# Two-layer hybrid decoder trunk on one core: the next layer's opening placed in the hand-made PE order of the last rows, the first stage reordered, the last products shared by ScalarE

## The chip, the cores and the metric

One core of one Trainium2 chip runs the whole program. The metric is the device time of the program in microseconds (us), lower is better. Engines: PE is TensorE, DVE is VectorE, ACT is ScalarE, POOL is GpSimd, SP is SyncE, which here only starts transfers.

## The reference

The trunk has DEPTH = 2 layers over a sequence of 512 tokens of 1024 float32 values (four tiles of 128 tokens). Each layer is, cut to its frame:

```
h = rms_norm(x, norm_g[l])
proj = h @ w_in[l]                      # 1024 -> 4376
q, k_c, v_c, k_s, v_s, k_w, v_w, g_lin, z_nsa, u_lru, z_lru, glu_a, glu_b, z_conv = split(proj)
gates = sigmoid(g_lin + b_gate[l])
y_nsa  = nsa_attention(...)             # compressed, selected and window branch, gated
y_lru  = rg_lru(...)
y_conv = conformer_conv(...)
mixed  = concat([y_nsa * silu(z_nsa), y_lru * silu(z_lru), y_conv * silu(z_conv)])
x = x + mixed @ w_out[l]                # 1536 -> 1024
```

and behind the second layer `rms_norm(x, final_g)` is the output. rms_norm is x / sqrt(mean(x*x) + 1e-6) * g over the 1024 values of a token.

## The kernel before

Matrices are multiplied in three products each: both operands are split in a high half (a cast by ACT, `cast` L149) and a low half (a subtraction by DVE, `lower` L152), and hi·hi, lo·hi and hi·lo are summed in one accumulator. So each weight tile takes a load (SP), a cast (ACT, tiles `whi`, `ow` or `wv`) and a subtraction (DVE, `wlo`, `ow` or `wv`) before all its products can run. All weights go through one pair of load buffers: `raw_tile` (L155) has two buffers of 1 MB, so a load waits until the casts and subtractions of the tile two places before it are done. SP starts its transfers in order.

**Opening of a layer** (L240 to L338): the weights of the values v_s, v_w and the gates are loaded (`wv`, 1024 rows in two pieces of 768 and 256 rows), split by `value_weights(j)` in parts j = 0, 1 (128x840) and 2 (128x560). Part 2 is kept in buffers that the queries (`QS`, tags qs0 and qs1) of the layer before used. Each token tile is normalised (`rms_norm` L220: squares on ACT with row sums, small sums on DVE, a power on POOL, a step of Newton's method on DVE, and the product with g), turned by eight PE transposes (`turned` L268, `hnat` to `H`, copied high by ACT and low by DVE), and multiplied by wv in 24 products (L321 to L338). In layer 0 the order of ACT and DVE in this stage is written out by hand in START (L44). In layer 1 the order is a scheduler's.

**End of a layer** (`last_rows`, L853): the attention of token tile 0 and the output products of the attention part for all tiles. The order of PE there is written out by hand in LAST_ROWS (L41): `s g b` are scores, `t g b` transposes of the weights P, `v g b` their products with the values, `o g` opens an output accumulator, and `r t n` are the 12 products of token tile t with half n of w_out (`out_rows` L417), added to x by DVE. The weights of half n are loaded and split where the first `r t n` of that half is met (`rows` L879, `out_weights` L406), so r30 stands for the load of half 0, r21 for that of half 1. The instructions of the other engines, and the places of loads in SP's queue, follow from the order in which the steps are written and from a scheduler. The opening of layer 1 was written behind all that, so its transposes and values came behind r00 on PE, but for what the scheduler moved.

**End of the program** (L922): each tile is normalised with final_g and stored; tile 0 is last, in two halves.

Of the kernel before, what the change touches and what calls it, by code (L numbers as in the profile page):

```python
# [1 line left out]

# [13 lines left out]
T = 512  # L16
# [21 lines left out]

LAST_ROWS = "s10 c s00 r30 s01 r20 d r10 t00 o0 t01 s11 v00 v01 r21 t10 t11 r31 o1 v10 v11 r11 r01 r00"  # L41


START = "q3 c3 p30 p31 q2 t30 c2 t31 p20 w0 p21 q1 t20 c1 w1 t21 p10 q0 p11 w2 t10 c0 t11 p00 p01 t00 t01"  # L44


@with_exitstack
def tile_hybrid_trunk(ctx, tc, x_in, positions, norm_g, w_in, b_gate, cmp_pos, cmp_w1, cmp_w2, lru_conv_w,
# [100 lines left out]
    def cast(out, in_):  # L149
        S.copy(out, in_)  # L150
# [58 lines left out]
                n += 1  # L209
        return p  # L210

    def rsqrt(y, v4):

        s = work.tile([128, 2], F32, name="nw", tag="nw", bufs=4)
        G.tensor_tensor(y, v4, power, op=OP.pow)  # L215
        V.tensor_scalar(s[:, 0:1], v4, -1.0, None, op0=OP.mult)
        V.scalar_tensor_tensor(s[:, 1:2], y, s[:, 0:1], y, op0=OP.mult, op1=OP.mult)
        V.scalar_tensor_tensor(y, s[:, 1:2], 3.0, y, op0=OP.add, op1=OP.mult)

    def rms_norm(x, gb, name, halves=False):  # L220

        y = pair(name)
        ss = work.tile([128, 4], F32, name="ss", tag="ss", bufs=4)
        for n in range(2):
            S.activation(y[:, n], x[:, n], AF.Square, accum_out=ss[:, n:n + 1])
            if n == 0:
                V.tensor_scalar(ss[:, 2:3], ss[:, 0:1], 4.0 / DM, 4.0 * EPS, op0=OP.mult, op1=OP.add)
        V.scalar_tensor_tensor(ss[:, 3:4], ss[:, 1:2], 4.0 / DM, ss[:, 2:3], op0=OP.mult, op1=OP.add)
        rsqrt(ss[:, 2:3], ss[:, 3:4])
        for n in (slice(0, 1), slice(1, 2)) if halves else (slice(0, 2),):  # L230
            V.scalar_tensor_tensor(y[:, n], x[:, n], ss[:, 2:3], gb[:, n], op0=OP.mult, op1=OP.mult)
        return y

    def load_g(ap):
# [2 lines left out]
        return g  # L237


    def layer(l, X):  # L240
        if l == 0:
            grow = pair("grow")[0:1].rearrange("p a c -> p (a c)")
            SP.dma_start(out=grow, in_=norm_g[0:1, :])
            load_x(0, X, (3, 2))
        else:
            gb = load_g(norm_g[l])
        wv = [w_cols(l, (COL["v_s"], 128), (COL["v_w"], 152), rows=rows) for rows in ((0, 6), (6, 2))]
        if l == 0:
            load_x(0, X, (1, 0))
        bg = work.tile([128, 24], F32, name="bg", tag="bg", bufs=1)  # L250
        SP.dma_start(out=bg, in_=bass.AP(tensor=b_gate.tensor, offset=b_gate[l].offset, ap=[[0, 128], [1, 24]]))

        def chan(name, src2d, n):
            t = main.tile([128, 4, n], F32, name=name, tag=name, bufs=1)
# [4 lines left out]
                PE.transpose(p[:, ct, :n], nat[:n, ct * 128:(ct + 1) * 128], ident[:n, :n])  # L259
            V.tensor_copy(t, p[:, :, :n])  # L260
            return t


        H2 = [[quad(f"H{w}{a}") for a in range(2)] for w in range(2)]
        Hh, Hl = [[H2[w][k // 4][:, k % 4, :] for k in range(8)] for w in range(2)]
        WV = [None] * 8

        def turned(t, h, n):  # L268
            p = psum.tile([128, 4, 128], F32, name="pt", tag="tr", bufs=2)
            for k in range(4):  # L270
                PE.transpose(p[:, k, :], h[:, n, k * 128:(k + 1) * 128], ident)
            sl = slice(t * 128, (t + 1) * 128)
            S.copy(H2[0][n][:, :, sl], p)
            V.tensor_tensor(H2[1][n][:, :, sl], p, H2[0][n][:, :, sl].bitcast(F32), op=OP.subtract)

        def value_weights(j):

            n = 3 if j < 2 else 2
            src = wv[j // 2][:, 3 * j % 6:3 * j % 6 + n, :]
            hi, lo = (main.tile([128, 4 if j == 2 else 2, 512], F32R, name="wv",  # L280
                                tag=(f"kh{j}", f"kl{j}")[w] if j < 2 else f"qs{w}", bufs=1) for w in range(2))
            hi, lo = (w.rearrange("p a b -> p (a b)")[:, :n * 280].rearrange("p (k c) -> p k c", k=n) for w in (hi, lo))
            cast(hi, src)
            lower(lo, src, hi)
            WV[3 * j:3 * j + n] = [(hi[:, k], lo[:, k]) for k in range(n)]

        if l == 0:

            hs, ss = {}, {}
            gp = [psum.tile([128, 512], F32, name="acc", tag="ps", bufs=3) for n in range(2)]  # L290
            for n in range(2):
                PE.matmul(gp[n], one, grow[:, n * 512:(n + 1) * 512], start=True, stop=True)

            def squares(t):
                hs[t] = pair("hnat")
                ss[t] = work.tile([128, 4], F32, name="ss", tag="ss", bufs=4)
                S.activation(hs[t], X[t], AF.Square, accum_out=ss[t][:, 0:1])

            def chain(t):
                V.tensor_scalar(ss[t][:, 3:4], ss[t][:, 0:1], 4.0 / DM, 4.0 * EPS, op0=OP.mult, op1=OP.add)  # L300
                rsqrt(ss[t][:, 2:3], ss[t][:, 3:4])

            def product(t, n):
                V.scalar_tensor_tensor(hs[t][:, n], X[t][:, n], ss[t][:, 2:3], gp[n], op0=OP.mult, op1=OP.mult)

            steps = dict(q=squares, c=chain, p=product, t=lambda t, n: turned(t, hs[t], n), w=value_weights)
            with tc.manual_schedule(engines={mybir.EngineType.Activation, mybir.EngineType.DVE}):
                for step in START.split():
                    steps[step[0]](*map(int, step[1:]))
        else:  # L310
            for j in range(3):
                value_weights(j)
            for t in (2, 3, 1, 0):
                SP.dma_start(out=saved[t], in_=X[t])
                h = rms_norm(X[t], gb, "hnat", t == 0)
                for n in range(2):
                    turned(t, h, n)


        VV, GT = [None] * 4, [None] * 4  # L320
        for t in (2, 3, 1, 0) if l else (3, 2, 1, 0):  # L321
            p = acc()
            sl = slice(t * 128, (t + 1) * 128)
            m = 0
            for k in range(8):
                for w, h in ((WV[k][0], Hh), (WV[k][0], Hl), (WV[k][1], Hh)):
                    PE.matmul(p[:, 0:280], h[k][:, sl], w, start=m == 0, stop=m == 23)  # L327
                    m += 1
            v = main.tile([128, 4, 2, 64], F32R, name="vv", tag="vv", bufs=4)
            pv = p[:, 0:256].rearrange("p (b d) -> p b d", b=4)  # L330
            S.copy(v[:, :, 0, :], pv)
            V.tensor_tensor(v[:, :, 1, :], pv, v[:, :, 0, :].bitcast(F32), op=OP.subtract)
            VV[t] = v
            gt = main.tile([128, 24], F32, name="gt", tag="gt", bufs=4)
            V.tensor_tensor(gt, p[:, 256:280], bg, op=OP.add)
            S.activation(gt, gt, AF.Tanh, scale=0.5)
            V.tensor_scalar(gt, gt, 0.5, 0.5, op0=OP.mult, op1=OP.add)
            GT[t] = gt  # L338


        dww = chan("dww", conv_dw_w[l], 31)
# [382 lines left out]
        def do_attn():  # L724
# [127 lines left out]

            def last_rows(X):  # L853
                new_mn(0)
                with tc.manual_schedule(engines={mybir.EngineType.PE}):
                    W, PTS, Ps, PO = {}, {}, {}, {}

                    def soft(g, b):
                        Ps[g, b] = weights_of(0, 4 * g, 4, b)

                    def turn(g, b):
                        PTS[g, b] = [big("pt", F32R).rearrange("p (k r q) -> p k r q", k=1, r=4) for _ in range(2)]
                        turned_weights(0, Ps[g, b], 4, PTS[g, b])

                    def comp():
                        PO["c"] = compressed_weights(0)

                    def turn_comp():
                        PO["c"] = turned_compressed(PO["c"])

                    def open_po(g):
                        PO[g] = new_po(g, PO["c"])

                    def vals(g, b):
                        values(PO[g], 0, g, b, PTS[g, b], b == 1)
                        if b == 1:
                            merged(PO[g], 0, g)

                    def rows(t, n):  # L879
                        if n not in W:  # L880
                            W[n] = out_weights(0, n, n == 1)
                        out_rows(X, t, n, W[n], MN[t])

                    steps = dict(s=soft, t=turn, c=comp, d=turn_comp, o=open_po, v=vals, r=rows)
                    for step in LAST_ROWS.split():
                        steps[step[0]](*map(int, step[1:]))

            return last_rows

# [22 lines left out]
        do_pw2()  # L912
        last_rows = do_attn()
        out_proj(X, 8, MC)
        last_rows(X)
        return X

    X = [None] * 4
    for l in range(DEPTH):
        X = layer(l, X)  # L920

    gb = load_g(final_g)  # L922
    for t in (2, 3, 1, 0):
# [31 lines left out]
```

## Time and profile before

| | us |
|---|---|
| median of 3 runs | 787.17 |
| lowest, highest | 785.59, 787.50 |
| the profiled execution, its own time | 786.09 |
| its span, first to last instruction | 784.3 |
| mean granted TensorE clock | 0.997 |

How to read it: the profile is one execution. A timeline row gives start, busy time, engine, line of the kernel, the operation, out<-in tiles (buffer numbers left out), the count of instructions that follow each other, and in brackets the idle time of the engine before the row with what ended it. Rows of PE overlap, since products are pipelined; from start to start is the measure of what they cost. A clock of 1.00 is 2.4 GHz, 0.50 is 1.2 GHz.

### The profile page before, as it was taken

Reading aid. Unit: us, or ns where it says so; the run is one execution under the profiler, and the core shown is the slowest. Engines: PE = TensorE matmul, PEld = TensorE weight load, DVE = VectorE, ACT = ScalarE, POOL = GpSimd, SP = SyncE. Lnnn points to the kernel's source line nnn. Section 1 sums busy time; section 2 is a strip of 40 time slices with the busy share of each in tenths; the row PEclk is TensorE's granted clock in tenths of the full one; section 3 lists DMA queues with packets and bytes.
Section 4 is the critical chain, followed back from the end, with each engine's and each line's share of the span. In section 5 each row is a group of like instructions: output and inputs, shape, how many; then the busy total and the mean of one; then the engine's idle time right before and its main releaser. Section 6 shows DMA issues by size and latency. Waiting matters only on the chain.

```text
span 784.3 us, 10943 instructions
## 1 busy us (share of the span) xinstructions
PE 755.0 (96%) x3816; PEld 604.8 (77%) x3816; DVE 676.4 (86%) x1243; ACT 452.1 (58%) x889; POOL 101.7 (13%) x179
## 2 busy tenths in 40 slices
PE   6999999999999999999989999999999999999995
PEld 4988887677887777888788888776788787778874
DVE  5889999999997788978873999999999778888766
ACT  5443666784336466667642348669534466676663
POOL 2000000000001132433210000000000103434240
PEclk9999999999999999999999999999999999999998
DMA  6433285656432200103531334771854140010002
GB/s 192 155 108 107 57 223 133 167 164 222 142 128 81 81 2 1 54 1 86 169 105 54 107 89 126 188 199 32 275 165 160 53 145 17 1 55 2 1 28 107
DMA packets 68245, 82.01 MB, mean 105 GB/s; under 512 B 6601, under 2 KB 56841, under 8 KB 68190
## 3 DMA queue, kind: packets, MB, share of 16 engines
q1 hardware_dynamic: 68190, 81.31, 33.9%
q8 instruction: 30, 0.49, 0.3%
q14 instruction: 25, 0.20, 0.1%
HBM read 67.67 MB, written 4.19 MB: 92 GB/s over the span
## 4 chain that ended last, share of the span: by engine, by line
PE 78%; DVE 9%; ACT 6%; issue 4%; POOL 2%; DMA 0%; POOLq 0%; DVEq 0%; SPq 0%; ACTq 0%
PE acc L208 43%; PE acc L423 10%; PE po L813 5%; PE pt L798 3%; PE acc L718 3%; PE acc L327 3%; PE ps L779 2%; ACT P L787 2%; PE ps L780 2%; DVE wlo L153 1%; DVE cv L381 1%; PE pt L630 1%; POOL P L791 1%; ACT pt L800 1%; PE pt L735 1%
## 5 line engine op out<-in xcount | busy, mean ns | idle before, releaser
L208 PE MATMUL acc<-H,whi 128*128 128x512 f32 x1024 | 325.5, 398 | 0.0
L208 PEld LDWEIGHTS acc<-H,whi 128*128 128x128 f32 x1024 | 191.1, 188 | 47.5 <-issue 1.9
L208 PE MATMUL acc<-H,wlo 128*128 128x512 f32 x512 | 203.7, 399 | 2.1 <-DVE wlo L153 2.1
L150 ACT CAST whi<-raw 128x1024 fp32r<-128x1024 f32 x102 | 106.5, 1050 | 159.4 <-PE acc L208 130.1
L381 DVE SCALAR_TENSOR_TENSOR cv<-sg,dww,cv 128x493 f32<-128x493 f32 (+18 forms) x240 | 165.9, 737 | 0.9
L153 DVE TENSOR_TENSOR wlo<-raw,whi 128x1024 fp32r<-128x1024 f32 x102 | 124.8, 1225 | 22.1 <-ACT whi L150 21.2
L208 PEld LDWEIGHTS acc<-H,wlo 128*128 128x128 f32 x512 | 96.2, 188 | 27.3 <-DVE wlo L153 3.4
L791 POOL TENSOR_SCALAR P<-P,hm,gt 128x384 f32<-128x384 f32 (+3 forms) x128 | 81.1, 643 | 135.7 <-DVE hm L789 127.1
L787 ACT ACTIVATE P<-ps,hm 128x384 f32<-128x384 f32 (+3 forms) x128 | 67.0, 532 | 15.7 <-DVE hm L784 15.1
L801 DVE TENSOR_TENSOR pt<-pt 128x512 fp32r<-128x512 f32 (+1 forms) x88 | 54.2, 638 | 12.9 <-ACT pt L800 11.8
L784 DVE TENSOR_REDUCE hm<-ps 128x1 f32<-128x384 f32 (+3 forms) x88 | 54.8, 634 | 8.2 <-PE ps L781 4.4
L813 PE MATMUL po<-pt,vv 128*128 128x256 f32 (+1 forms) x304 | 58.0, 304 | 1.1 <-DVE pt L801 0.7
L215 POOL TENSOR_TENSOR mv<-mv,power 128x1 f32<-128x1 f32 x8 | 4.2, 544 | 418.1 <-DVE mv L680 418.1
L800 ACT CAST pt<-pt 128x512 fp32r<-128x512 f32 (+1 forms) x88 | 46.0, 548 | 21.4 <-PE pt L798 18.8
L813 PEld LDWEIGHTS po<-pt,vv 128*128 128x128 f32 x304 | 44.7, 189 | 9.8 <-ACT pt L800 4.6
L798 PE MATMUL pt<-ident,P 128*128 128x128 f32 x320 | 47.6, 275 | 1.6 <-POOL P L791 1.3
L779 PE MATMUL ps<-KH,QS 128*128 128x384 f32 (+3 forms) x128 | 45.5, 367 | 0.8 <-ACT P L787 0.6
L798 PEld LDWEIGHTS pt<-ident,P 128*128 128x128 f32 x320 | 36.9, 140 | 6.0 <-POOL P L791 4.1
L780 PE MATMUL ps<-KL,QS 128*128 128x384 f32 (+3 forms) x128 | 40.5, 328 | 0.0
L327 PE MATMUL acc<-wv,H 128*128 128x280 f32 x192 | 30.6, 313 | 2.5 <-ACT wv L150 1.5
L425 DVE TENSOR_TENSOR x<-x,acc 128x512 f32<-128x512 f32 x48 | 32.4, 677 | 0.8 <-PE acc L423 0.4
L423 PE MATMUL acc<-whi,mn 128*128 128x512 f32 x96 | 31.1, 406 | 0.0
(233 smaller groups left out, 1213.3 us busy)
## 6 DMA issues: line engine op xcount, KB each, us to landing
raw<-in_w_in_dram SPq DMA_DIRECT2D x30, 1024.0 KB
raw<-in_w_out_dram SPq DMA_DIRECT2D x12, 1024.0 KB
raw<-in_cmp_w_dram SPq DMA_DIRECT2D x8, 1024.0 KB
x<-in_x_dram SPq DMA_DIRECT2D x8, 512.0 KB
raw<-in_w_in_dram SPq DMA_DIRECT2D x4, 512.0 KB
QS<-rs SPq DMA_DIRECT2D x8, 256.0 KB
QS<-ru SPq DMA_DIRECT2D x8, 256.0 KB
KH<-rs SPq DMA_DIRECT2D x8, 256.0 KB
```

The lines of the kernel that those rows point to most:

```text
L150: S.copy(out, in_)
L153: (eng or V).tensor_tensor(out, in_, hi.bitcast(F32), op=OP.subtract)
L208: PE.matmul(p, w[k], h[k], start=n == 0, stop=n == 23)
L381: V.scalar_tensor_tensor(a[:, s:], u[:, :T - s], dww[:, ct, j:j + 1], a[:, s:], op0=OP.mult, op1=OP.add)
L423: PE.matmul(p, h[:, k], w, start=m == 0, stop=m == 11)
L779: PE.matmul(sc[:, r, :], q, KH[g][:, b, :L], start=r == 0, stop=False)
L780: PE.matmul(sc[:, r, :], q, KL[g][:, b, :L], start=False, stop=False)
L784: V.tensor_reduce(hm[:, 0, :nh], sc, axis=AX.X, op=OP.min)
L787: S.activation(P[:, r * L:(r + 1) * L], sc[:, r, :], AF.Exp, scale=-1.0, bias=hm[:, 0, r:r + 1], accum_out=hm[:, 1, r:r + 1])
L791: G.tensor_scalar(P[:, r * L:(r + 1) * L], P[:, r * L:(r + 1) * L], hm[:, 2, r:r + 1], GA[i][:, h0 + r, 1 + b:2 + b], op0=OP.mult, op1=OP. ...
L798: PE.transpose(pt[:, kb, :], P[:, kb * 128:(kb + 1) * 128], ident)
L813: PE.matmul(po, v, PT[w][:, kb].rearrange("p r q -> p (r q)"), start=False, stop=last and kb == i and w == 1)
```

## The change

- LAST_ROWS has the opening of the next layer in it: `L` are its loads, `W` the splits of wv, `N t` the norm of tile t, `T t` its eight transposes, `V t` its 24 products. The functions of the opening move into `opening`, which hands these steps to `last_rows` of layer 0. In layer 1 there is no next layer, and the new steps are skipped.
- START is reordered and its step c (row sums and root) is split in c and e; in layer 0, x of tile 3 is loaded first, g by ACT's queue, and wv in three pieces, of 384, 384 and 256 rows.
- rms_norm of the last tile of a norm: squares of half 1 first; x·g of half 1 is made before the root is known, and ACT multiplies it by the root while DVE makes half 0.

```diff
-LAST_ROWS = "s10 c s00 r30 s01 r20 d r10 t00 o0 t01 s11 v00 v01 r21 t10 t11 r31 o1 v10 v11 r11 r01 r00"
-START = "q3 c3 p30 p31 q2 t30 c2 t31 p20 w0 p21 q1 t20 c1 w1 t21 p10 q0 p11 w2 t10 c0 t11 p00 p01 t00 t01"
+LAST_ROWS = "s10 c s00 r30 s01 r20 d r10 t00 o0 t01 s11 L v00 v01 r21 N2 t10 W t11 r31 N3 o1 v10 v11 T2 r11 N1 r01 " \
+            "T3 r00 N0 V2 T1 V3 T0 V1 V0"
+START = "q3 c3 e3 p30 p31 q2 c2 w0 e2 t30 p20 t31 q1 p21 c1 w1 e1 t20 p10 t21 q0 p11 c0 w2 e0 t10 p00 t11 p01 t00 t01"
...
-    def rms_norm(x, gb, name, halves=False):
+    def rms_norm(x, gb, name, last=False):
...
-        for n in range(2):
+        for n in ((1, 0) if last else (0, 1)):
             S.activation(y[:, n], x[:, n], AF.Square, accum_out=ss[:, n:n + 1])
-            if n == 0:
-                V.tensor_scalar(ss[:, 2:3], ss[:, 0:1], 4.0 / DM, 4.0 * EPS, op0=OP.mult, op1=OP.add)
+            if n == last:
+                V.tensor_scalar(ss[:, 2:3], ss[:, n:n + 1], 4.0 / DM, 4.0 * EPS, op0=OP.mult, op1=OP.add)
+                if last:
+                    V.tensor_tensor(y[:, 1], x[:, 1], gb[:, 1], op=OP.mult)
...
-        for n in (slice(0, 1), slice(1, 2)) if halves else (slice(0, 2),):
-            V.scalar_tensor_tensor(y[:, n], x[:, n], ss[:, 2:3], gb[:, n], op0=OP.mult, op1=OP.mult)
+        n = slice(0, 1 if last else 2)
+        V.scalar_tensor_tensor(y[:, n], x[:, n], ss[:, 2:3], gb[:, n], op0=OP.mult, op1=OP.mult)
+        if last:
+            S.activation(y[:, 1], y[:, 1], AF.Copy, scale=ss[:, 2:3])
...
+    def opening(l, X):
...
+        def loads():
+            load_wv(0, 6)
+            load_wv(6, 2)
+            o.gb = load_g(norm_g[l])
+            load_bg()
...
+        if l:
+            o.steps = dict(L=loads, W=weights, N=norm, T=turned_tile, V=values)
+            return o
...
+        load_x(0, X, (3,))
+        grow = pair("grow")[0:1].rearrange("p a c -> p (a c)")
+        S.dma_start(out=grow, in_=norm_g[0:1, :])
+        load_x(0, X, (2,))
+        load_wv(0, 3)
+        load_wv(3, 3)
+        load_x(0, X, (1, 0))
+        load_wv(6, 2)
+        load_bg()
...
             def last_rows(X):
                 new_mn(0)
+                nxt = opening(l + 1, X) if l + 1 < DEPTH else None
...
                     steps = dict(s=soft, t=turn, c=comp, d=turn_comp, o=open_po, v=vals, r=rows)
+                    if nxt:
+                        steps |= nxt.steps
                     for step in LAST_ROWS.split():
-                        steps[step[0]](*map(int, step[1:]))
+                        if step[0] in steps:
+                            steps[step[0]](*map(int, step[1:]))
+                return nxt
```

SP's queue at the end of layer 0. Before (lines of the kernel before); 128x4x512 is a half of w_out, 6x128 and 6x152 are the first piece of wv, 2x128 and 2x152 the second, 8x256 the first weights of layer 1's projection:

```order
L409 DMA raw<-in_w_out_dram 128x4x512 x4
L708 DMA pwr<-in_conv_w_pw_dram 128x2x256 x2
L409 DMA raw<-in_w_out_dram 128x4x512
L708 DMA pwr<-in_conv_w_pw_dram 128x2x256 x2
L409 DMA raw<-in_w_out_dram 128x4x512
L165 DMA raw<-in_w_in_dram 128x6x128
L165 DMA raw<-in_w_in_dram 128x6x152
L236 DMA g<-in_norm_g_dram 128x1024
L165 DMA raw<-in_w_in_dram 128x2x128
L165 DMA raw<-in_w_in_dram 128x2x152
L165 DMA raw<-in_w_in_dram 128x8x256 x2
```

The same place with the change:

```order
L447 DMA raw<-in_w_out_dram 128x4x512 x4
L746 DMA pwr<-in_conv_w_pw_dram 128x2x256 x2
L447 DMA raw<-in_w_out_dram 128x4x512
L746 DMA pwr<-in_conv_w_pw_dram 128x2x256 x2
L168 DMA raw<-in_w_in_dram 128x6x128
L168 DMA raw<-in_w_in_dram 128x6x152
L168 DMA raw<-in_w_in_dram 128x2x128
L168 DMA raw<-in_w_in_dram 128x2x152
L251 DMA g<-in_norm_g_dram 128x1024
L447 DMA raw<-in_w_out_dram 128x4x512
L168 DMA raw<-in_w_in_dram 128x8x256 x2
```

The load of the second half of w_out, which r21 to r01 read, stood ahead of both pieces of wv and now stands behind them.

ACT in the same place, before; `whi` and `ow` here are the two casts of that second half:

```order
L150 CAST whi<-raw 128x1024
L800 CAST pt<-pt 128x512
L828 CAST mn_3162<-m 128x256
L800 CAST pt<-pt 128x512
L150 CAST ow<-raw 128x1024
L824 COPY oe<-po 64x256
```

and with the change, where the casts of that half stand behind those of wv and ahead of the squares of the next norm:

```order
L153 CAST wv<-raw 128x560
L153 CAST wv<-raw 128x840
L862 COPY oe<-po 64x256
L825 ACTIVATE P,hm<-ps,hm 128x128 x4
L862 COPY oe<-po 64x256
L866 CAST mn_3537<-m 128x256
L153 CAST whi<-raw 128x1024
L153 CAST ow<-raw 128x1024
L236 ACTIVATE hnat,ss<-x_1867 128x512
```

The two casts (and DVE's two subtractions with them) were done in the middle of the attention of tile 1; now they stand at the place of r21.

PE behind the last product of r00, before:

```order
L271 MATMUL pt<-ident,hnat 128x128 x6
L327 MATMUL acc<-wv,H_3868 128x280
L271 MATMUL pt<-ident,hnat 128x128 x4
L327 MATMUL acc<-wv,H_3870 128x280
L327 MATMUL acc<-wv,H_3868 128x280
L271 MATMUL pt<-ident,hnat 128x128 x4
```

and with the change, from the output products of tile 1 on, at the step T3:

```order
L461 MATMUL acc<-ow,mn_3537 128x512
L278 MATMUL pt<-ident,hnat 128x128 x8
L461 MATMUL acc<-whi,mn_3537 128x512
L461 MATMUL acc<-whi,mn_3538 128x512
L461 MATMUL acc<-wlo,mn_3537 128x512
```

Transposes of tiles 2 and 3 now stand among output products, and each tile's values run as one group of 24.

## Rows read from the trace of the kernel before

**Rows 1.** The page: busy time of each engine, share, instructions

```profile
PE 755.0 (96%) x3816; PEld 604.8 (77%) x3816; DVE 676.4 (86%) x1243; ACT 452.1 (58%) x889; POOL 101.7 (13%) x179
```

**Rows 2.** Timeline of PE at the layer boundary (columns as told above)

```profile
375.80 1.28 PE L813 MATMUL po<-pt,vv 128*128 128x512 f32 x4
376.91 0.62 PE L423 MATMUL acc<-whi,mn 128*128 128x512 f32 x2
...
379.69 1.72 PE L798 MATMUL pt<-ident,P 128*128 128x128 f32 x7
381.67 0.33 PE L798 MATMUL pt<-ident,P 128*128 128x128 f32 x1 [0.26 <-POOL P L791]
...
394.52 0.82 PE L271 MATMUL pt<-ident,hnat 128*128 128x128 f32 x6
396.23 0.40 PE L327 MATMUL acc<-wv,H 128*128 128x280 f32 x1 [0.89 <-ACT H L273]
397.88 0.66 PE L271 MATMUL pt<-ident,hnat 128*128 128x128 f32 x4 [1.25 <-DVE H L274]
...
401.07 0.60 PE L271 MATMUL pt<-ident,hnat 128*128 128x128 f32 x4
401.43 1.78 PE L327 MATMUL acc<-wv,H 128*128 128x280 f32 x12
403.40 0.66 PE L271 MATMUL pt<-ident,hnat 128*128 128x128 f32 x4 [0.18 <-DVE H L274]
...
405.13 8.41 PE L327 MATMUL acc<-wv,H 128*128 128x280 f32 x63
```

**Rows 3.** Timeline of SP's queue: the load of w_out's second half

```profile
315.13 0.37 SPq L409 DMA_DIRECT2D raw<-in_w_out_dram  x1
```

**Rows 4.** Timeline of DVE: the last two subtractions of wv

```profile
376.42 0.74 DVE L153 TENSOR_TENSOR wv<-raw,wv 128x560 fp32r<-128x560 f32 x1
...
378.01 1.01 DVE L153 TENSOR_TENSOR wv<-raw,wv 128x840 fp32r<-128x840 f32 x1
```

**Rows 5.** Stretches: us, busy by engine, PEclk, DMA share, GB/s

```profile
315.13:320.10 4.97, 4.96 (x33) 3.77 (x32) 4.52 (x11) 3.89 (x10) 2.87 (x4) 1.00 0.67 214
```

**Rows 6.** Groups by form: busy us, mean ns | idle before

```profile
L153 DVE TENSOR_TENSOR wlo<-raw,whi 128x1024 fp32r<-128x1024 f32 x102 | 124.8, 1225 | 22.1 <-ACT whi L150 21.2
L150 ACT CAST whi<-raw 128x1024 fp32r<-128x1024 f32 x102 | 106.5, 1050 | 159.4 <-PE acc L208 130.1 <-issue 19.8 <-PE acc L423 6.5
...
L273 ACT CAST H<-pt 128x512 fp32r<-128x512 f32 x16 | 9.3, 584 | 11.7 <-PE pt L271 11.5
```

**Rows 7.** Stretches at the end of the program

```profile
770.00:779.60 9.60, 6.94 (x30) 5.11 (x28) 7.04 (x18) 2.58 (x7) 1.41 (x3) 1.00 0.27 109
779.60:784.30 4.70, 0.00 (x0) 0.00 (x0) 1.67 (x4) 0.00 (x0) 0.00 (x0) 0.50 0.29 113
```

**Rows 8.** Timeline of PE: the longest wait in mid-program

```profile
165.22 0.38 PE L630 MATMUL pt<-wlo,cMs 128*124 128x256 f32 x1 [1.47 <-DVE wlo L153]
```

**Rows 9.** Timeline of PE in the first stage

```profile
11.56 0.83 PE L327 MATMUL acc<-wv,H 128*128 128x280 f32 x2 [1.47 <-ACT wv L150]
13.13 1.08 PE L271 MATMUL pt<-ident,hnat 128*128 128x128 f32 x4 [0.73 <-DVE hnat L304]
...
16.25 4.33 PE L327 MATMUL acc<-wv,H 128*128 128x280 f32 x24
20.41 0.60 PE L271 MATMUL pt<-ident,hnat 128*128 128x128 f32 x4
```

**Rows 10.** Timeline of all engines at the end

```profile
776.55 0.40 PE L423 MATMUL acc<-wlo,mn 128*128 128x512 f32 x1
...
776.98 0.69 DVE L425 TENSOR_TENSOR x<-x,acc 128x512 f32<-128x512 f32 x1
...
778.64 0.16 DVE L228 SCALAR_TENSOR_TENSOR ss<-ss 128x1 f32<-128x1 f32 x1
...
779.93 1.42 DVE L231 SCALAR_TENSOR_TENSOR o<-x,ss,g 128x512 f32<-128x512 f32 x2
```

More of the change, by code (lines that the diff above doesn't have):

```diff
@@ L1 @@
 from contextlib import ExitStack
+from types import SimpleNamespace
 import concourse.bass as bass
@@ L210, in proj, with root_seed @@
         return p
-    def rsqrt(y, v4):
+    def root_seed(y, v4):
         s = work.tile([128, 2], F32, name="nw", tag="nw", bufs=4)
@@ L253, in chan, with layer @@
+    def layer(l, X, o):
+        Hh, Hl, VV, GT = o.Hh, o.Hl, o.VV, o.GT
         def chan(name, src2d, n):
@@ L261, in chan @@
             return t
[L264 to L308, printed above, removed]
-                    steps[step[0]](*map(int, step[1:]))
[L310 to L317, printed above, removed]
@@ L320, in layer @@
[L320 to L338, printed above, removed]
@@ L884, in last_rows @@
                     steps = dict(s=soft, t=turn, c=comp, d=turn_comp, o=open_po, v=vals, r=rows)
+                    if nxt:
+                        steps |= nxt.steps
                     for step in LAST_ROWS.split():
-                        steps[step[0]](*map(int, step[1:]))
+                        if step[0] in steps:
+                            steps[step[0]](*map(int, step[1:]))
+                return nxt
             return last_rows
@@ L914, in layer @@
         out_proj(X, 8, MC)
-        last_rows(X)
-        return X
+        return X, last_rows(X)
     X = [None] * 4
+    o = opening(0, X)
     for l in range(DEPTH):
-        X = layer(l, X)
+        X, o = layer(l, X, o)
     gb = load_g(final_g)
```

88 lines of the change are left out of this document (75 added, 13 removed).

## The prediction

> **What bounds the kernel now.** Read the page first: TensorE (PE) is busy for 96% of the span [rows 1], so a change counts only where it moves PE's stalls, its clock, or the tail behind its last product. Three stretches are touched, and I read each in the timeline of PE, then asked the engine behind each stall.
>
> The layer boundary comes first. In its rows the reader is to compare starts, not busy times: the last of eight transposes begun at 379.69 starts at 381.67, 1.98 us later; four need 0.36 us from start to start (401.07 to 401.43), so seven need 0.63, and 1.35 us were a wait for POOL's P. The other brackets are ACT's and DVE's copies of H: 0.89 before 396.23, 1.25 before 397.88, 0.18 before 403.40 [rows 2]. From start to start these three cost a little more. Six transposes from 394.52 are done by 395.06 and the next product starts 1.17 us later. It takes 0.13 us (63 such products in 8.41 us), so the 397.88 row starts 1.52 us late. The third costs 0.37, from 12 products begun at 401.43. Together **4.4 us of stall** stand between the last rows of layer 0 and the first projection of layer 1.
>
> Second, the queue of loads. The second w_out tile of the last rows (call it W1, 1 MB) was issued at 315.13, more than 60 us before its first use at 376.91 [rows 2, 3]; the weights of the next opening (wv) stood behind it in the queue. Third come the start and the end, below.
>
> **The boundary: what is removed.** The hand order now holds all four turned tiles and all values of layer 1. Each T stands a product group or more ahead of the V that reads it, so the three H stalls (3.06 us) should vanish. The wait for P at t10 and t11 (1.35) vanishes too, but only because PE will be waiting for something longer just before. The sum of removals is −4.4 us.
>
> **The boundary: what is added.** The order of the SP queue shows it. L is emitted ahead of r21, and r21 is the first step that asks for W1. There are two raw buffers. Before, W1 took its buffer first and wv came after; now both wv tiles take them first and W1 is last of the three. Its load must wait until DVE has done the subtraction of the 128x560 part of wv. That instruction ran at 376.42 for 0.74 us, so until 377.16, and cannot come earlier: its output lies in the query tiles that the scores of s11 read, and PE ran those directly ahead of v00, which began at 375.80 [rows 2, 4]. PE finishes v00 and v01 at 377.1 (375.80 + 1.28) and has r21 next in a fixed order. So the whole load is now exposed. The load issued at 315.13 moved 214 GB/s on average for 4.97 us, which is the whole tile [rows 5]; so W1 lands at 377.16 + 4.97 = 382.1. ACT's cast takes 1.05 [rows 6]: 383.2. Before, r21 began at 376.91 without a wait. **The wait is 6.3 us.** Two products later (0.46 us) PE needs the low half, which DVE makes in 1.22 us [rows 6] from 383.2, so until 384.4: 0.8 more. Queued behind W1's casts on ACT, in the new order, are the squares of the next norm, and on DVE the sums of squares; I follow them through the rows' durations and find one new wait, of 0.5, for the low half of tile 0's merged rows before r01. The boundary at unchanged clock: 6.3 + 0.8 + 0.5 − 4.4 = **+3.2 us**.
>
> **The clock.** At the end of the program PE's last product ends at 776.95 [rows 10], the granted clock is 1.00 up to 779.6 and 0.50 behind it [rows 7], that is 1.2 GHz, after 2.65 us of idle PE. The longest wait in the middle that the trace shows, 1.47 us, ahead of 165.22 [rows 8], has no such drop. The new idle is 6.3 us, so I take the first row: PE comes back at the low level. What that costs is read at the start, where PE works without a bracket from 13.13 on. Four transposes take 1.08 us at 13.13 and 0.60 at 20.41; the 24 products from 16.25 to 20.41 took 4.16 us where 24 at 0.133 take 3.2 [rows 9]. At twice 0.133 each, 7 of them ran slow, until about 18.1. So 5 us of work ran at half rate and lost 2.5 us. After the wait 0.8 us of the slow stretch is idle anyway (the low half of W1 is missing), which leaves **+1.7**; bounds 0 and +2.5. The Trainium skill, "TensorE: Matmul & The Clock Gate", section "HAM oscillation — how this bites in real kernels", says that a long wait for a transfer in mid-kernel throttles TensorE, and that the work behind it starts slow; by it this term is paid in full, by the 1.47 us row alone it is nothing. The 0.50 at the end agrees with the page; no row before shows it in mid-program.
>
> **The start.** ACT's cast of the first wv part moves ahead of the first copies of H, and DVE's root and products are cut finer. PE's idle of 1.47 before 11.56, which that cast ended, and of 0.73 before 13.13 [rows 9] can go, 2.2 us, but what runs then runs at half rate, so it is worth 1.1. Against it, the last tile's eight transposes now stand directly ahead of the first projection product, which waits for ACT's two copies behind them, about 1.2 us at 0.58 each [rows 6]. These cancel: +0.1. If the clock rises earlier because PE starts its unbroken work earlier by 2.2 to 2.8 us, half of that is won, −1.1 to −1.4. I take −0.7, between the two, with bounds −1.7 and +0.3. The third piece of wv now waits for a raw buffer that the first returns; 18 products of each tile stand ahead of those that read it, and I cost it at nothing; if that cover is too short, it is part of the +0.3.
>
> **The end.** Behind the last product (776.95) the chain is x add, square, two small sums, root, and two multiplications in 1.42 us [rows 10]. Half of the last (0.7) goes to ACT beside DVE, and one small sum of 0.16 leaves the chain; the early x·g on DVE, as long as an x add (0.69), can delay the last x add by up to 0.3. **−0.5**, bounds −0.7 and 0. In the last layer the hand order has no new steps.
>
> **Sum:** 3.2 + 1.7 − 0.7 − 0.5 = **+3.7 us**. On the profiled execution, 786.09, that is 789.8. That run is 1.1 below the median 787.17 of three (785.59 to 787.50), on which it would be 790.9. I write 790.3. About 0.3%, 2.4 us, can be told from no change.
>
> **Rivals.**
> - *The clock holds through the wait.* For it: no mid-program drop in the trace. Against it: the 0.50 at the end. Then +2.0, so 788.1 to 789.2; with the whole gain at the start +1.0, 787.1. Within 0.3%. Chance 0.22.
> - *Worse than forecast.* The next 1 MB w_in load is released by DVE's 128x840 subtraction, which ended 1.9 us after the 128x560 one [rows 4]; sharing the transfer engines it could take 0.9 us from W1, the clock may cost its 2.5, and squares delayed behind W1's casts could keep one H stall (1.2). Together up to +6.6, 793. For it: the new order puts both in flight together. Against it: the second has a start 1.9 us later, and the first is over in 5. Chance 0.12. The skill's "DMA: Bandwidth & Descriptors", section "Two DMAs through the same engine are not ordered", says that transfers of one queue start in order; by that the 0.9 would be nearly nothing. No row here separates two such loads.
> - *Faster.* W1's load is no longer last, because the earlier stretch has lost W1's two casts and two subtractions on ACT and DVE (4.5 us of work by [rows 6]), and the wv subtraction comes well ahead of PE's v01. The sum without clock loss is the wait − 4.3 (0.8 + 0.5 − 4.4 − 0.7 − 0.5), so it decides for the other side below a wait of 1.9 us; at no wait at all the 0.8 goes too: −5.1, 782. Against it: the wv subtraction is tied to the scores that stand right before v00 on PE, so both move together. Chance 0.10.
>
> **How the numbers follow.** The forecast itself has 0.56 (788.9 to 792.5). Slower by over 0.3% (above 789.5): 0.55 of it and the worse case, 0.67. Faster 0.10. The rest, 0.23, is the same. The range 786.9 to 793.4 takes in the second and most of the third case and leaves out the faster one.
>
> **What would show it.** In the profile of the changed kernel: PE idle for about 6 us before the first product of r21 (the line of out_rows), released by ACT's cast of w_out; W1's load issued right behind DVE's 128x560 subtraction; a granted clock below 1.00 in the 10 us behind that; no brackets before the transposes and values of tiles 2, 3, 1, 0; the distance from PE's last product to the end of the span shorter than 7.35 us by 0.5. A wait under 2 us there, or no such wait, would prove the argument wrong, as would 1.00 throughout for its clock term.

## The result

The changed kernel takes **790.76 us** (median of 6 runs, 790.19 to 791.22), the kernel before 787.12 us beside it (6 runs, 785.32 to 787.50). The ratio is 1.0052, 95% interval 1.0039 to 1.0065: slower by 0.5%, clear of noise. The forecast was 790.3 us, the range 786.9 to 793.4.

The profiled execution took 790.41 us, its span is 788.7 us, 4.4 more than before's. Where they arose, by the start of the same piece of work in both profiles:

| point | before | after | later by |
|---|---|---|---|
| second projection group of layer 0, second product | 37.45 | 37.28 | −0.2 |
| v00 in the last rows of layer 0 | 375.80 | 374.75 | −1.05 |
| first projection product of layer 1 | 414.06 | 418.27 | +4.2 |
| end of the last product | 776.9 | 781.2 | +4.3 |
| end of the span | 784.3 | 788.7 | +4.4 |

All the loss lies in some 40 us at the layer boundary. From v00 to the first product of layer 1 the changed kernel needs 43.5 us and the kernel before 38.3, so 5.3 us were lost there; 1.05 had been won on the way to v00. The first product of layer 1 in the timelines of PE, before and after:

```profile
414.06 0.72 PE L208 MATMUL acc<-H,whi 128*128 128x512 f32 x2
```

```profile
418.27 0.72 PE L211 MATMUL acc<-H,whi 128*128 128x512 f32 x2
```

The timeline of PE in the changed kernel, at the boundary, which answers to [rows 2]; the columns are the same:

```profile
374.75 1.28 PE L851 MATMUL po<-pt,vv 128*128 128x512 f32 x4
382.47 1.22 PE L461 MATMUL acc<-whi,mn 128*128 128x512 f32 x2 [6.44 <-ACT whi L153]
383.73 0.79 PE L461 MATMUL acc<-wlo,mn 128*128 128x512 f32 x1
...
387.83 1.03 PE L836 MATMUL pt<-ident,P 128*128 128x128 f32 x8
388.62 0.71 PE L461 MATMUL acc<-whi,mn 128*128 128x512 f32 x2
...
397.95 1.86 PE L461 MATMUL acc<-ow,mn 128*128 128x512 f32 x6
399.65 1.04 PE L278 MATMUL pt<-ident,hnat 128*128 128x128 f32 x8
...
403.32 3.29 PE L305 MATMUL acc<-wv,H 128*128 128x280 f32 x24
406.45 1.04 PE L278 MATMUL pt<-ident,hnat 128*128 128x128 f32 x8
...
411.26 6.48 PE L305 MATMUL acc<-wv,H 128*128 128x280 f32 x48
```

One bracket is left in the whole boundary, and it is new: PE waits 6.44 us for ACT's cast of the second half of w_out. None of the waits of [rows 2] is there any more: transposes and values follow one another without a bracket. The cause of the new wait, in SP's queue, on DVE and on ACT (three timelines of the changed kernel):

```profile
376.15 0.37 SPq L447 DMA_DIRECT2D raw<-in_w_out_dram  x1
```

```profile
375.38 0.74 DVE L156 TENSOR_TENSOR wv<-raw,wv 128x560 fp32r<-128x560 f32 x1
```

```profile
381.37 1.04 ACT L153 CAST whi<-raw 128x1024 fp32r<-128x1024 f32 x1 [1.30 <-DMA raw<-in_w_out_dram]
382.32 1.04 ACT L153 CAST ow<-raw 128x1024 fp32r<-128x1024 f32 x1
```

The load, issued at 315.13 before [rows 3], is issued at 376.15, where DVE's 128x560 subtraction ends (375.38 + 0.74); ACT casts its data 5.2 us later. The description of the kernel before says that a load waits for the tile two places before it, which here would be the 768-row piece of wv, not split until 377.98 (128x840). The issue at 376.15 fits only the buffer of the 256-row piece, which stands directly ahead of W1 and is split first. The clock in three stretches around it (us, busy time of PE, PEld, DVE, ACT and POOL with counts, PEclk, DMA share, GB/s):

```profile
374.70:380.60 5.90, 1.33 (x7) 0.78 (x6) 4.80 (x9) 4.09 (x13) 1.93 (x4) 1.00 0.47 174
380.60:387.40 6.80, 4.89 (x11) 3.40 (x12) 2.49 (x4) 3.23 (x6) 0.25 (x1) 0.50 0.69 210
387.40:395.00 7.60, 7.50 (x42) 6.11 (x41) 5.28 (x14) 3.78 (x11) 0.71 (x2) 1.00 0.57 211
```

PE had been idle since 376.03 when the granted clock fell to 0.50, 1.2 GHz, at 380.6; the products of r21 ran at that level.

The first stage and the end did not gain. In the first stage DVE stands still where it did not before, and PE behind it. DVE's cast of the positions (L126 before, L129 after) has moved ahead of the last subtraction of wv (128x560). The timeline of DVE, before and after, and then that of PE in the changed kernel, to be held against [rows 9]:

```profile
19.46 0.73 DVE L153 TENSOR_TENSOR wv<-raw,wv 128x560 fp32r<-128x560 f32 x1
...
22.34 0.42 DVE L126 CAST ang<-pi 128x512 f32<-128x512 int32 x1
```

```profile
18.80 0.43 DVE L129 CAST ang<-pi 128x512 f32<-128x512 int32 x1 [1.98 <-DMA pi<-in_positions_dram]
...
19.21 0.73 DVE L156 TENSOR_TENSOR wv<-raw,wv 128x560 fp32r<-128x560 f32 x1
```

```profile
16.76 0.60 PE L278 MATMUL pt<-ident,hnat 128*128 128x128 f32 x4
...
19.99 1.68 PE L305 MATMUL acc<-wv,H 128*128 128x280 f32 x11 [0.64 <-DVE wv L156]
```

PE reached full rate by 16.76 (four transposes in 0.60 us; before at 20.41), and gave it back waiting for the third part of wv. At the end, the x add behind the last product starts 0.5 us late, because the early x·g sits ahead of it (all engines, to be held against [rows 10]; PE ends at 781.2):

```profile
781.11 0.68 DVE L240 TENSOR_TENSOR o<-x,g 128x512 f32<-128x512 f32 x1
781.71 0.68 DVE L463 TENSOR_TENSOR x<-x,acc 128x512 f32<-128x512 f32 x1
...
784.44 0.72 ACT L246 ACTIVATE o<-o,ss 128x512 f32<-128x512 f32 x1 [1.30 <-DVE ss L225]
784.44 0.75 DVE L244 SCALAR_TENSOR_TENSOR o<-x,ss,g 128x512 f32<-128x512 f32 x1
```

The two last multiplications now run side by side, and their chain from PE's end takes 4.0 us instead of 4.4, but both stores are ready together and go one behind the other through SP. From PE's last product to the end of the span it is 7.46 us, before 7.40.

### The profile page after: what moved, and what is told of

The parts are those of the page before. It is cut to its first block, busy times and chain, and to the rows that moved or that the text cites. A ratio compares the mean times of both kernels' runs of the same rounds, so it can differ in the third digit from the quotient of the medians.

```text
span 788.7 us, 10946 instructions
## 1 busy us (share of the span) xinstructions
PE 756.4 (96%) x3816; PEld 606.3 (77%) x3816; DVE 675.3 (86%) x1243; ACT 454.1 (58%) x891; POOL 102.8 (13%) x179
## 4 chain that ended last, share of the span: by engine, by line
PE 79%; DVE 9%; ACT 5%; issue 3%; DMA 2%; POOL 2%; POOLq 0%; DVEq 0%; ACTq 0%
PE acc L211 43%; PE acc L461 11%; PE po L851 5%; PE pt L836 4%; PE acc L756 3%; PE ps L817 2%; PE acc L305 2%; PE ps L818 2%; DVE cv L419 1%; DVE wlo L156 1%; ACT P L825 1%; PE pt L668 1%; DMA raw<-in_w_in_dram 1%; POOL P L829 1%; ACT pt L838 1%
```

## The experiments

The theory: the late load of W1 (the second half of w_out) is the loss, its wait with the low clock behind it; the dense order itself is a gain. Rivals: the interleaving is the loss; the load would be hidden anyway. Twelve kernels ran in three groups, the second on another chip than the first and the third, each group with the kernel before beside it: medians 786.09, 785.98 and 785.45 us. Beside the changed kernel it was 787.12, so times compared across groups can be off by over 1 us. A sharper measure is the distance in a profile from v00 to the first product of layer 1, the boundary:

| kernel | boundary, us |
|---|---|
| before | 38.3 |
| changed | 43.5 |
| changed, old first stage (experiment 2) | 43.0 |
| the two with the filler (experiment 2) | 41.9, 41.6 |
| L behind r21, opening interleaved (seven kernels) | 35.0 to 35.1 |
| opening behind the rows, L ahead of r21, behind it (experiment 3) | 50.3, 42.1 |

**1. The place of L.** One step of the hand order is moved, so that W1 takes its buffer ahead of both pieces of wv.

```diff
-s11 L v00 v01 r21 N2 t10 W ...
+s11 v00 v01 r21 L N2 t10 W ...
```

> The changed kernel with one step moved: L stands behind r21 in the hand order, so the load of the second half of w_out (W1) is queued ahead of both wv pieces again. Theory (the late load is the loss): the 6.4 us wait of PE ahead of r21 and the 0.5 us for its low half are gone, the granted clock stays 1.00 through the boundary, the wait for P at the transposes of t10 and t11 (1.35 us) is back, the three H stalls of before (3.06 us) stay away; the boundary is 3 us shorter than before's instead of 4.8 longer, so about 783 to 784 us. Rival (the interleaved order itself costs: transposes and norms among the rows delay ACT and DVE): new waits at T and V take the place of the load's, and the time stays above 787. Rival (the load is hidden anyway, the clock is what costs): no change of the wait, 790.

Measured: 784.00 us (10 runs), ratio 0.9974 (0.9963 to 0.9985). In its timeline of PE (five rows at the boundary), r21 starts without a bracket and the wait for P is back; the clock is 1.00 throughout:

```profile
377.50 1.27 PE L851 MATMUL po<-pt,vv 128*128 128x512 f32 x4
378.62 0.62 PE L461 MATMUL acc<-whi,mn 128*128 128x512 f32 x2
...
381.37 1.77 PE L836 MATMUL pt<-ident,P 128*128 128x128 f32 x7
383.40 0.33 PE L836 MATMUL pt<-ident,P 128*128 128x128 f32 x1 [0.26 <-POOL P L829]
...
412.57 0.72 PE L211 MATMUL acc<-H,whi 128*128 128x512 f32 x2
```

Against before, v00 comes 1.7 us later and the first product of layer 1 1.5 earlier: the boundary is 3.2 us shorter, where the theory gave 3.06. The theory holds on this point, and the change turns from slower to faster by one step. The 1.7 us ahead of the boundary arose in the first stage, which ended 2.1 late in this profile (experiment 4).

**2. The clock behind the wait.** 26 products on data that is there fill the wait; nobody reads their sum.

```diff
-s11 L v00 v01 r21 N2 ...
+s11 L v00 v01 f r21 N2 ...
...
+def fill():
+    p = psum.tile([128, 512], F32, name="ps", tag="ps", bufs=3)
+    for i in range(26 if nxt else 0):
+        PE.matmul(p.rearrange("p (r k) -> p r k", r=4), identb, maskb.unsqueeze(1).to_broadcast([128, 4, 128]),
+                  start=i == 0, stop=i == 25)
...
```

> The changed kernel with 26 products (the score mask's operands, 128x512, their sum read by nobody) put on PE between v01 and r21, to fill the wait and nothing else. Theory: the wait for W1 stays (first product of r21 at the same 382.5 us), but PE is not idle for 6 us, the granted clock stays 1.00, and what stands behind the wait runs at full rate: from the first product of r21 to the first behind t10 and its eight transposes 6.15 us in the changed kernel, about 4.2 here; so about 2 us faster than the changed kernel, 788.5 to 789. Rival (the clock is of no weight): 790.8 as the changed kernel. Rival (the products behind the wait are slow because of the low half and ACT, not the clock): the clock reads 1.00 and the 6.15 us stay.

Measured: 790.37 us (4 runs), ratio 1.0057 (1.0038 to 1.0076): as a time, no different from the changed kernel's 1.0052, so the expected 2 us did not show. The four times lie in two pairs, 789.53 and 789.61, 791.13 and 791.52; the profiled one is the fastest. In its timeline of PE most of the gain is there:

```profile
376.53 5.79 PE L926 MATMUL ps<-maskb,identb 128*128 128x512 bf16 x26
383.49 0.74 PE L461 MATMUL acc<-whi,mn 128*128 128x512 f32 x2 [1.17 <-ACT whi L153]
384.75 0.50 PE L461 MATMUL acc<-wlo,mn 128*128 128x512 f32 x1 [0.53 <-DVE wlo L156]
...
387.18 1.04 PE L836 MATMUL pt<-ident,P 128*128 128x128 f32 x8
387.97 0.71 PE L461 MATMUL acc<-whi,mn 128*128 128x512 f32 x2
```

From r21's first product to the end of the eight transposes it is 4.48 us (383.49 to 387.97), in the changed kernel 6.15 (382.47 to 388.62): 1.67 us. The boundary costs 3.6 us against before, not 5.3. Part of that gain was lost again in the first stage, which was 0.4 us slower than before's in this run and 0.2 faster in the changed kernel's profile; why two of the four runs are slower still is not shown. So the pair was run again with the first stage of before (START and the loads of layer 0), where this stage is steadier:

```diff
-START = "q3 c3 e3 p30 p31 q2 c2 w0 e2 t30 p20 t31 q1 p21 c1 w1 e1 t20 p10 t21 q0 p11 c0 w2 e0 t10 p00 t11 p01 t00 t01"
+START = "q3 c3 e3 p30 p31 q2 t30 c2 e2 t31 p20 w0 p21 q1 t20 c1 e1 w1 t21 p10 q0 p11 w2 t10 c0 e0 t11 p00 p01 t00 t01"
...
-        load_wv(0, 3)
-        load_wv(3, 3)
+        load_wv(0, 6)
+        load_wv(6, 2)
         load_x(0, X, (1, 0))
-        load_wv(6, 2)
```

> The changed kernel (L ahead of r21) with the first stage put back as before the change: differs from the run with the old first stage and L behind r21 by the place of one step alone. Theory: the 6.4 us wait before r21, 0.5 us for its low half and the low clock behind it are all back, the P wait of 1.35 us goes: 7 to 8 us slower than that run (782.65), 789.5 to 790.7. Rival (the first stage and its clock, not the late load, make up part of the changed kernel's loss): under 6 us slower, below 788.7.

> The run before this one, with 26 products between v01 and r21 that fill the wait (their sum is read by nobody). Theory: the granted clock stays 1.00 through the boundary, the wait for the load stays; 1.7 us faster than the run without them (the 1.67 us by which the stretch from r21's first product to the end of the next eight transposes was shorter in the first filler run). Rival (the clock is of no weight in the end): within 0.5 us of it.

Measured: 790.52 us without the filler (5 runs, 789.89 to 790.99), 789.11 with it (5 runs, 788.49 to 789.65): the ranges do not meet, 1.4 us. In the profiles the boundary is shorter by the same 1.4; the profiled runs differ by 2.0, of which 0.9 had arisen before v00, so this stage varies too. The clock fell to 0.50 at 380.1 without the filler and reads 1.00 with it (its two stretches, the products of the filler and what follows):

```profile
375.40:382.00 6.60, 5.88 (x28) 2.46 (x26) 3.71 (x8) 4.00 (x14) 2.17 (x4) 1.00 0.77 257
382.00:387.00 5.00, 4.36 (x22) 3.40 (x23) 3.17 (x5) 2.81 (x8) 0.00 (x0) 1.00 0.54 162
```

So the low clock is worth 1.4 to 1.7 us of the loss, and the wait itself the larger part.

**3. Interleaved or behind.** The four norms, transposes and values are taken out of the rows and put in hand order behind r00, with L ahead of r21 or behind it.

```diff
-s11 L v00 v01 r21 N2 t10 W t11 r31 N3 o1 v10 v11 T2 r11 N1 r01 T3 r00 N0 V2 T1 V3 T0 V1 V0
+s11 L v00 v01 r21 t10 W t11 r31 o1 v10 v11 r11 r01 r00 N2 T2 N3 T3 N1 T1 V2 N0 V3 T0 V1 V0
```

and for the second kernel

```diff
-s11 L v00 v01 r21 t10 W ...
+s11 v00 v01 r21 L t10 W ...
```

> The changed kernel with L where it is (ahead of r21), but norms, transposes and values of the next layer in hand order behind r00 (W behind t10 stays): takes the interleaving away and keeps the late load. Theory (the late load is the loss): the wait of about 6.4 us before r21 and the low clock behind it stay; time within 1.5 us of the changed kernel, 790 to 792. Rival (interleaving is the loss): the wait shrinks or the time falls to 787 or below.

> As the run before this one (opening in hand order behind r00), with L behind r21: takes both the interleaving and the late load away. Theory: no wait at r21, clock 1.00, the P wait of 1.35 us at t10 and t11 as in the kernel before; about 783.5 to 785.5, so that the four orders (L ahead of or behind r21, opening among or behind the rows) differ by 6 to 8 us with the place of L and by under 1.5 us with the interleaving. Rival (interleaving is what counts): the place of L makes less than 2 us.

Measured: 799.41 us (1.0167, 1.0147 to 1.0186) and 789.83 us (1.0049, 1.0031 to 1.0067). Both expectations missed by far. By the boundaries in the table, the place of L makes 8.2 us here and 8.5 in the interleaved order; the interleaving makes 7.0 us with L behind r21 and 6.8 with L ahead. (The times give 9.6 and 6.8, 5.8 and 8.6, with the changed kernel's taken from another group.) The timeline of PE of the second kernel, behind r00, shows why, and so do two stretches of it:

```profile
394.39 1.03 PE L278 MATMUL pt<-ident,hnat 128*128 128x128 f32 x8
397.29 0.66 PE L278 MATMUL pt<-ident,hnat 128*128 128x128 f32 x4 [1.86 <-DVE H L281]
399.09 1.97 PE L278 MATMUL pt<-ident,hnat 128*128 128x128 f32 x8 [1.15 <-DVE H L281]
401.61 1.12 PE L278 MATMUL pt<-ident,hnat 128*128 128x128 f32 x4 [0.55 <-DVE H L281]
402.37 7.92 PE L305 MATMUL acc<-wv,H 128*128 128x280 f32 x48
```

```profile
394.40:398.80 4.40, 1.68 (x13) 1.20 (x11) 4.40 (x8) 3.38 (x8) 1.42 (x2) 1.00 0.29 119
398.80:405.60 6.80, 5.96 (x26) 5.56 (x27) 5.05 (x10) 2.38 (x4) 0.98 (x3) 0.50 0.49 154
```

Three tiles' transposes stand in a row with nothing between them, so each waits for DVE's copy of the one before (two buffers for what PE has turned), and then the clock falls too. So two things of the change are shown at once: the interleaving is its gain, and the late load its loss. The 7 us are measured against an order that is worse than before's, though: in the rows of before the tiles' transposes were mixed with values, and they waited less. Against before the interleaving gains the 3.2 us of experiment 1.

**4. The first stage.** Three kernels, all with L behind r21: the first stage put back; the positions loaded ahead of the third piece of wv; wv in two pieces, so that SP never waits for a buffer there.

The edit of the first is that of experiment 2. The second (`load_positions` holds the loads of inv and pi, taken out of `rope_tables`) and the third:

```diff
         load_x(0, X, (1, 0))
+        o.pos = load_positions()
         load_wv(6, 2)
```

```diff
-        load_wv(3, 3)
+        load_wv(3, 5)
         load_x(0, X, (1, 0))
-        load_wv(6, 2)
```

> The kernel with L behind r21, and the first stage put back: the order of START, the order of the loads and the two wv pieces as before the change. Theory (the new first stage is no gain, because DVE's first instruction of the rope tables, the cast of the positions, now stands ahead of the third wv subtraction and waits about 2 us for a load that SP issues late, behind the third wv piece): PE's wait of 0.6 to 1.1 us before the values that read that part is gone, the second projection group starts within 0.2 us of before's 37.45, and the time is no worse than the run with L behind r21, 783.0 to 784.0 (beside 784.0 there). Rival (the new first stage gains the 0.7 us of the prediction): 0.7 us slower than that run, 784.7 or more.

> The kernel with L behind r21, and the loads of inv and the positions put ahead of the third wv piece in SP's queue; nothing else. Theory: DVE's 2 us wait for the positions is gone and with it PE's wait before the third wv part (0.6 to 1.1 us); the second projection group starts 0.7 to 1.1 us earlier than with the new first stage (39.6 or 37.3 in the profiles so far, whether the clock fell in the stage or not), at about 36.5; 0.7 us faster than the run with L behind r21, more where that lost its clock. Rival (the third piece's own load is late, behind its buffer): PE's wait stays within 0.2 us of what it was.

> The kernel with L behind r21, and in layer 0 wv loaded in two pieces of 3 and 5 row blocks, so that no wv load waits for a buffer and SP is not held; the positions stay where they are in the queue. Theory: SP is not held at the third piece (1.6 us), but the small rows ahead of the positions and the queue's own pace stay, so DVE's wait for the positions shrinks by 0.5 to 1.5 us and PE's wait by as much; gain of 0.3 to 1 us over the run with L behind r21. Rival (buffer and queue are not what makes the positions late): nothing changes in that wait.

Measured: 782.65 us (0.9952, 0.9934 to 0.9971), 785.04 us (0.9988, 0.9979 to 0.9997), 784.64 us (0.9978, 0.9967 to 0.9989). By these times the old first stage is 1.35 us better than the new, as the theory said. Two other pairs differ by the first stage alone and show less: 790.76 against 790.52 (changed kernel, experiment 2), 782.58 against 782.25 (experiment 5). In the profiles the second projection group's second product stands at 37.3 to 39.6 in seven kernels with the new stage (40.2 with the positions loaded ahead) and at 36.3 to 37.5 in five with the old. So the new stage gains nothing; it comes out worse in each comparison of times, in two of them by less than the runs spread, and how much it loses is not settled. The two repairs failed. In the third the cast of the positions waited 2.31 us, no less than before the repair. In the second it came earlier in DVE's order, along with its load, and waited longer (timeline of DVE):

```profile
12.63 0.43 DVE L132 CAST ang<-pi 128x512 f32<-128x512 int32 x1 [4.61 <-DMA pi<-in_positions_dram]
```

and PE waited 5.0 us for a low half behind it. So it is the place of that cast on DVE, not the buffer, that matters; in the changed kernel the load of the positions was even issued a little earlier than before (14.45 against 15.14). The run of experiment 1 had another loss in this stage, which its stretches show in the clock:

```profile
20.00:25.60 5.60, 3.77 (x24) 2.80 (x24) 5.07 (x13) 3.39 (x6) 0.00 (x0) 1.00 0.81 266
25.60:29.10 3.50, 3.50 (x17) 3.48 (x16) 3.47 (x11) 1.61 (x4) 0.00 (x0) 0.51 0.05 16
```

After waits of 1.06, 0.27, 0.63 and 0.22 us the clock fell, and the stage ended 2.1 us behind before's. Its ten runs lie in two groups, 782.87 to 783.34 and 784.65 to 784.89; the profiled one is of the upper.

The last kernel on this point writes the rope tables behind the glu projection (with L behind r21 and the end of experiment 5), so that the cast is gone from the stage; its timeline of PE stands behind the edit's expectation:

```diff
-if l == 0: rope_tables()
 do_glu()
+if l == 0: rope_tables()
```

> L behind r21, the new first stage, the two queues at the end, and the rope tables written behind the glu projection, so that no cast of the positions stands in DVE's hand order of the first stage. Theory (that cast and its wait are what spoilt the new first stage): PE's wait before the third wv part (0.6 to 1.6 us) is gone, the clock does not fall again in the stage, the second projection group starts at 36.3 to 36.8 instead of 37.3 to 39.6; about 0.7 us faster than old_stage_two_queues, 781.6, unless the tables' 6 us of DVE work stall the projections later. Rival (the new order of the stage is itself the worse one): the second group starts at 37.2 or later.

Measured: 786.77 us (1.0021, 1.0011 to 1.0032), slower, where 781.6 was expected. But the stage does what it was meant to, more than expected: PE has no bracket but two of 0.9 and 0.4 us at its head, and the second group's second product at 34.57, 2.9 us ahead of before.

```profile
18.72 2.31 PE L305 MATMUL acc<-wv,H 128*128 128x280 f32 x16
20.87 1.04 PE L278 MATMUL pt<-ident,hnat 128*128 128x128 f32 x8
21.66 6.46 PE L305 MATMUL acc<-wv,H 128*128 128x280 f32 x48
...
28.64 0.72 PE L211 MATMUL acc<-H,whi 128*128 128x512 f32 x2
```

But v00 starts at 381.18, 5.4 us behind before's, so 8.3 us are lost on the way, most of them between 130 and 220 us. Among them are waits for DVE (`wlo`, 3.8 us in four) and one low-clock stretch of 3.4 us; that the tables' DVE work is what delays these is likely and was not shown.

**5. The end.**

```diff
-V.tensor_tensor(y[:, 1], x[:, 1], gb[:, 1], op=OP.mult)
+G.tensor_tensor(y[:, 1], x[:, 1], gb[:, 1], op=OP.mult)
...
-SP.dma_start(out=out[0, ...], in_=o[:, c[0]:c[1]])
+(S if c[0] else SP).dma_start(out=out[0, ...], in_=o[:, c[0]:c[1]])
```

> The kernel with L behind r21, and at the end x*g of the last tile's second half on POOL instead of DVE, and its store issued by ACT instead of SP. Theory (the end gained nothing because x*g held the last x add for 0.5 us on DVE and both stores, ready at once, are issued one behind the other on SP): the last x add starts 0.03 us behind PE's last product instead of 0.5, the last store is issued 0.8 to 0.9 us earlier relative to it; the distance from PE's last product to the end of the span falls from 7.4 to about 6.5 us. Rival (the span's end is set by the write of the stores, whatever they wait for): the distance stays above 7.1 us.

> L behind r21, the first stage as before the change, x*g of the last tile's second half on POOL and its store issued by ACT. The two gains add if they are independent: 782.65 less 0.3 (the tail was 7.12 us with the two queues, 7.4 to 7.6 without), about 782.3. Rival (the tail's gain was chance): 782.6 or more with a tail above 7.4 us.

Measured: 782.58 us (0.9958, 0.9945 to 0.9970) with the new first stage, and **782.25 us** (0.9957, 0.9944 to 0.9969) with the old. The x add no longer waits (0.03 us behind PE's end), though POOL takes 2.2 us for the product that DVE makes in 0.68. The tail, from PE's last product to the end of the span, is 7.12 us with the new stage and 7.28 with the old, against 7.45 and 7.57 in the same kernels with one queue: a gain of 0.3 us, not of 0.9. The last store starts 0.8 us earlier, but the span ends 3.5 and 3.7 us behind it instead of 3.1 and 3.2, so the rival has half of the truth. 782.25 is 0.4 below the run with the old first stage, within the spread of their runs. It is the lowest median: 3.2 us ahead of the kernel before beside it and some 8 ahead of the changed one; 782.58 and 782.65 cannot be told from it.

## Why the prediction was right

- **The wait for W1** (forecast 6.3 us). The bracket is 6.44 in the changed kernel, 6.23 with the old first stage; by starts, as the forecast counts, the changed kernel's is 6.6. The load's issue follows the 128x560 subtraction to a few hundredths. With one step moved, [rows 2]'s start of r21 without a wait is back (experiment 1). On its own, with the clock and the low half, the place of L is worth 7.9 us, by the boundaries (43.0 against 35.1) and by the times (790.52 against 782.65, two groups). The load took 5.2 us from issue to cast where 4.97 were forecast, so the 0.9 of the rival in which a second load takes its share was not paid.
- **The low half** (0.8). With full clock (experiment 2) its bracket is 0.53, and by starts it costs 0.80: the product that reads it starts 1.26 us behind r21's first, where two products need 0.46. In the changed kernel slow products cover most of it, as its place in the clock term had it.
- **The clock** (1.7, bounds 0 and 2.5): 1.67 by the two stretches, 1.4 by the times. It fell while PE had been idle since 376.03 and came back at 387.4. The rival in which it holds is out. The Trainium skill's section "HAM oscillation — how this bites in real kernels" of "TensorE: Matmul & The Clock Gate" had spoken for the fall in mid-program, and this trace agrees with it: 0.50 from 380.6 to 387.4.
- **The stalls removed** (4.4): the H stalls are gone, and the wait for P goes only where PE waits for W1. With W1 early the boundary gains 3.2 us, against 3.06 forecast for the H stalls.
- **The new wait at r01** (0.5): its six `ow` products, at 397.95, take 1.70 us to the next row instead of 1.4; 0.3 us, without a bracket. At the same place of before they took 1.59 (390.14 to 391.73), so only 0.1 is new.
- **The start** (−0.7, bounds −1.7 and +0.3): this step failed. I took the reordered stage to be PE's and ACT's affair and costed the third wv piece at nothing; the cover was there for its load, but not for DVE, whose order had taken in the cast of the positions ahead of the third subtraction. Measured: −0.2 in the changed kernel's profile, +0.4 to +2.1 in six other profiles with the new stage, and 0.2 to 1.35 us worse than the old stage by three pairs of times. Without that cast the stage gains 2.9 us, which is beyond my bound on the other side.
- **The end** (−0.5): this step was off too. The delay of the x add was 0.5, not 0.3, and I had not asked which queue the stores leave by. The tail grew by 0.06.
- **Ahead of v00** 0.5 us came unforecast, between the middle of layer 0 and v00; ACT and DVE have lost W1's splits there. That these are the cause was not tested. Together with a drift of 0.4 us over the projections it makes up for the two terms that failed, so the sum, +3.7 forecast and +4.4 in the profiles' spans, is closer than its parts. The mechanism at the boundary was right (+4.9 forecast, +5.3 measured). The start and the end were to give −1.2; outside the boundary −0.9 came, most of it from another place, and that was luck.

## What to carry to other kernels

Where a step in a hand-made order also asks for a buffer, as r21 does here, its place in the text decides who gets the buffer: list the loads in queue order before and after, and for each the instruction that frees its buffer. Interleave producers that wait for other engines (transposes and their copies) with long products, and look then at every other engine's order for instructions that slipped in between, with the load that each of them waits for. The wait of 6.4 us cost its own length and 1.4 to 1.7 us of slow products behind it. A sum that comes out right can hide terms that failed: hold each term against its own stretch of the profile.

## What was not expected of the hardware

The granted clock fell without one long idle stretch. In the kernel with the opening behind the rows and L behind r21 it went to 0.50 at 398.8, after a wait of 1.86 us and within the next, of 1.15, both among transposes. In the first stage of experiment 1 it fell after waits of 1.06, 0.27, 0.63 and 0.22 us, for 3.4 us. But the size of the waits does not tell when: in the kernel of experiment 5 with the new first stage the same four waits were 1.57, 0.27, 0.63 and 0.23 us, and the clock stayed at 1.00 (timeline of PE, and a stretch to be held against the one in experiment 4):

```profile
20.79 1.68 PE L305 MATMUL acc<-wv,H 128*128 128x280 f32 x11 [1.57 <-DVE wv L156]
```

```profile
25.60:29.10 3.50, 3.50 (x29) 3.46 (x28) 3.49 (x11) 1.68 (x5) 0.00 (x0) 1.00 0.09 29
```

In the kernel before it stayed up too, through waits of 0.89, 1.25 and 0.18 us with values between them [rows 2] and the single one of 1.47 us [rows 8]. What tells these cases apart was not tested.
